# Three units of FFN2's weight sums on GpSimd in the chunk loop, and an eighth pair of strips by the seven-product scheme

## The chip, the cores and the metric

The kernel runs on one core of a Trainium2 chip. The metric is the device time of one execution in microseconds (us), as the median of several runs. TensorE (PE in the profile) multiplies, VectorE (DVE) and ScalarE (ACT) work on whole tiles, GpSimd (POOL) does a few small operations, and SyncE (SP) issues nearly all DMA transfers, in the order of its queue.

## The reference

One layer of a hybrid decoder over 1024 tokens with 1024 channels, all in float32: a SwiGLU half-step, a mixer of three parallel branches (an RWKV-7 recurrence, sliding-window attention, cross-attention into memory tokens) merged by gates, and a second SwiGLU half-step.

```python
def swiglu(u, w_in, w_out):
    gate, up = jnp.split(u @ w_in, 2, axis=-1)
    return (jax.nn.silu(gate) * up) @ w_out

f1 = swiglu(rms_norm(h, ffn1_pre_g[l]), ffn1_w_in[l], ffn1_w_out[l])
h = h + HALF_STEP * rms_norm(f1, ffn1_post_g[l])
u = rms_norm(h, mix_pre_g[l])
p_rwkv, p_swa, q_mem, gate_logits = _split(u @ w_in[l], IN_SIZES)
y_a = rwkv7_mix(p_rwkv, ...)
y_b = sliding_window_gqa_sinks(q_s, k_s, v_s, swa_sinks[l])
y_c = memory_cross_attention(q_mem.reshape(B, S, MEM_HEADS, MEM_HEAD_DIM), mem_n, mem_w_kv[l])
g_a, g_b, g_c = _split(jax.nn.sigmoid(gate_logits + gate_b[l]), (D, D, D))
merged = (g_a * (y_a @ w_branch[l, 0]) + g_b * (y_b @ w_branch[l, 1])
          + g_c * (y_c @ w_branch[l, 2]))
h = h + rms_norm(merged @ w_out[l], mix_post_g[l])
f2 = swiglu(rms_norm(h, ffn2_pre_g[l]), ffn2_w_in[l], ffn2_w_out[l])
h = h + HALF_STEP * rms_norm(f2, ffn2_post_g[l])
```

## The kernel before

**Products.** Every float32 matrix product is made of three matmuls on operands that are split in a high and a low part (`mm3`, L378 to L380): high by high, high by low, low by high. A weight tile (`w_raw`, 128x512, loaded by SP at L292) is split by a cast on ACT (`w_hi`, L301) and a subtraction on DVE (`w_lo`, L303). `plan` lists all weight operands in the order of use, and each is loaded and split some tiles ahead.

**The seven-product scheme.** A strip is 128 output columns of a projection. A plain strip takes 2 token halves x 8 blocks of 128 channels x 3 matmuls (`gate_block`, PSUM banks `pgate`). `win_pair` makes two strips at once by a Strassen-like scheme: 7 products of 4 blocks each on sums of the input (`mix_form`, products t1 to t4) and of the weights, on the banks `px`, `py` and `pz`, with `kept` copying partial sums to SBUF on ACT (`part`, L1437). `WIN_PAIRS` lists the pairs. FFN1 and FFN2 use such schemes too; for FFN2's output weights the sums of the weights are made in 11 units (q = 0 to 10) of four tiles: four loads, four DVE operations (L669 to L672), four stores to `ffn_sum_d` (`sums_beside`, on tiles named `gin`). A unit is taken up by `unit()` at the end of a gate in `filling`.

**The stages around the change.** The mixer's strips are projected, the last of them in pairs. Then comes the chunk loop of the recurrence (`rwkv_chain`, 16 chunks of 64 tokens), whose small matmuls depend on each other; gates 10 and 11 fill PE's gaps there. For each chunk SP loads `f` (640 KB) and `dinv`, POOL copies part of `f` into `gz` (L1230) and multiplies the state by the chunk's decay (`sw`, L1297), PE makes `z`, DVE copies it out of PSUM (`z`, `uv`) and makes the next state (`ts`, then `sv` at L1314 out of `ts` and `sw`). The dictionary `beside` puts further loads on SP behind the `dinv` loads of a chunk: the memory attention's `km`, `vm` and `qm`. `rwkv_finish` normalises the recurrence's output (squares `ysq` on POOL, `yrs`, `gup`). Then the memory attention runs in 8 blocks (`MemoryBlock`: scores `msc`, maxima and sums `mst` on DVE, exponentials `mp` on ACT, transposes `mptr` on PE), and the window attention; `filling` gives gates 12 to 23 and then the branch products (`pb`, weights `in_wb`) to PE wherever an attention block waits. The branch inputs are loaded as `yin` and split into `y` on ACT and DVE; the last branch's are loaded behind its window blocks.

**What sets the order.** A recording layer writes each engine's queue in one order ahead of time. `issue_after(x)` puts an instruction behind x in that order, `high_priority` ahead of others, and `keep_in_program_order` holds it to the code's. Within an engine's queue nothing overtakes.

Of the kernel before, what the change touches and what calls it, by code (L numbers as in the profile page):

```python
# [11 lines left out]
F32 = mybir.dt.float32  # L12
F32R = mybir.dt.float32r
I32 = mybir.dt.int32
ALU = mybir.AluOpType
# [3 lines left out]
P = 128  # L19
# [8 lines left out]
KP = KF // 2  # L28
OUT_FORMS = (("b11", 0), ("b21", 1), ("t2", "s2"), ("t3", "s3"), ("t4", 3), ("t1", "s1"), ("b22", "s4"))
B_FORM = {b: i for i, (b, _) in enumerate(OUT_FORMS)}  # L30
SUMS = ("s1", "s2", "s3", "s4")
# [7 lines left out]
NPAIR = 4  # L39
MAIN_PSUM = ("po", "px", "py", "pr", "pgate", "pq", "pb", "pw")  # L40
OPS = 8
KEEP = KP - OPS
RAWS = 5
SCRATCH = 1024
FORM_TILES = {"ffn1": 8, "ffn2": 12}
KH = KD // 2
# [3 lines left out]
CORNER = (4, 4)  # L50
GATES_FIRST = 10
GATES_EARLY = 12
LUMPS = (29, 52)
# [8 lines left out]
C = 64  # L62
# [170 lines left out]
class Builder:  # L233
# [430 lines left out]
    def sums_made(self, f, q, a, behind):  # L664
# [8 lines left out]
        for n, t in zip(SUMS, (a22, a11, a21, a12)):  # L673
            nc.sync.dma_start(self.sum_d[f][SUMS.index(n), q], t)

    def sums_beside(self):

        for q in range(KP):
            a = [t[:, i * TH : (i + 1) * TH].rearrange("p (k c) -> p k c", c=P) for t in (self.wide(), self.wide()) for i in (0, 1)]
            self.sums_loads("ffn2", q, a)  # L680
            yield
            self.sums_made("ffn2", q, a, self.split_last)

    def unit(self):
        if self.units:
            next(self.units, None)
# [521 lines left out]

    def rwkv_chain(self, pool, early, fetched, pk_d, inv_d, y, beside):
        nc = self.nc  # L1210
        V, S, G = nc.vector, nc.scalar, nc.gpsimd
        lo, hi = slice(0, 64), slice(64, 128)
        ROWS = (lo, hi)
# [6 lines left out]
        tile = lambda tag, shape, bufs=2: pool.tile([P] + shape, F32, tag=tag, name=tag, bufs=bufs)  # L1220
# [52 lines left out]
        n = load(0)  # L1273
# [7 lines left out]
        for c in range(NC_):  # L1281
            last = c == NC_ - 1
            nxt = None if last else load(c + 1)
            if c in beside:
                with self.tc.issue_after(self.asked.ins):
                    beside[c]()
            wc = self.wc[:, c, :].rearrange("p n -> p n ()")

            ps = self.psum("z")
            for p, q in pairs:  # L1290
                q = 1 - q
# [4 lines left out]
            for q in (0, 1):  # L1296
                G.tensor_tensor(sw[ROWS[q]], n["sv"][ROWS[q], q], wc[ROWS[q]].broadcast_to([64, NPAIR, C]), ALU.mult)  # L1297
            py = out(c - 1, before) if c else self.psum("y")
# [5 lines left out]
            if not last:  # L1304
# [3 lines left out]
                for p, q in pairs:  # L1308
                    q = 1 - q
# [179 lines left out]
    def filling(self, u, pool, gate_d, y_d):  # L1489

        for g in range(GATES_EARLY, 22):
            ps = {h: self.psum("pgate") for h in (0, 1)}
            yield from self.project_steps(self.strip("win", 24 + g), u, ps)
            self.gate_out(g, ps, pool, gate_d)
            self.unit()

# [259 lines left out]
    def mixer(self, u, cp, close_raws, att_d, gate_d, km_d, vm_d):  # L1756
# [23 lines left out]
        with tc.tile_pool(reuse_waits="tile", name="gates", bufs=2) as gp:  # L1780
# [33 lines left out]
            blocks = [MemoryBlock(self, None, b, att_d=att_d, km=km, vm=vm, ahead=ahead, y_d=y_d[2]) for b in range(nb)]  # L1814
            beside = {3: lambda: nc.sync.dma_start(km, km_d), 5: lambda: nc.sync.dma_start(vm, vm_d), 7: blocks[0].load, 8: blocks[1].load}
            with chunks, tc.tile_pool(reuse_waits="tile", name="chain", bufs=2) as pool:
                y = pool.tile([P, NPAIR, T], F32, name="y", bufs=1)
                last = self.rwkv_chain(pool, early, fetched, pk_d, inv_d, y, beside)
                with tc.issue_after(self.opened.ins):
                    for g in range(GATES_FIRST, GATES_EARLY):  # L1820
                        self.gate_block(g, u, gp, gate_d)
                self.held = []
                self.fills, self.missing = self.filling(u, gp, gate_d, y_d), 0
                self.fill(8, self.solved)
                last()
                self.rwkv_finish(pool, early, y, bonus_d, y_d[0])
            with stay, tc.tile_pool(reuse_waits="tile", name="att", bufs=1) as ap, tc.tile_pool(name="attw", bufs=2) as pool:
# [261 lines left out]
```

## Time and profile before

| | |
|---|---|
| median of 3 runs | 2253.84 us (2252.64 to 2255.07) |
| the profiled execution | 2256.49 us, its span 2254.8 us |
| mean granted TensorE clock | 0.997 |
| PE busy | 2227.1 us, 99% |
| DVE busy | 1642.5 us, 73% |
| ACT busy | 1029.6 us, 46% |
| POOL busy | 81.3 us, 4% |

The span runs from the first to the last instruction of the profiled execution. Busy times are shares of that span. In a timeline a row has the start, the length, the engine, the line and the operation with output and inputs, a count of like neighbours (x2), and in brackets the time the engine stood before it and what released it. In the list of waits stand engine and line, what was waited for, the time in us, how often, and the longest.

### The profile page before, as it was taken

The numbers are of one execution on the slowest core, as the hardware profiler recorded it, in microseconds if no ns is written. First come the engines' busy times: TensorE is split into PE (matmuls) and PEld (weight loads), VectorE is DVE, ScalarE is ACT, GpSimd is POOL, SyncE is SP. The second block draws the span as 40 slices with busy tenths as digits, with TensorE's granted clock in tenths as the row PEclk, the third lists the DMA queues.
The fourth block names the chain that finished last, engine by engine and source line by source line (L and its number), as shares of the span: only waits on it lengthen the run. The fifth ranks groups of instructions, "written<-read, shape, count | busy, mean of one in ns | idle before, by whom it ended". The sixth has DMA issues, their size and how long they took to land.

```text
span 2254.8 us, 34592 instructions
## 1 busy us (share of the span) xinstructions
PE 2227.1 (99%) x12304; PEld 1830.2 (81%) x12304; DVE 1642.5 (73%) x2761; ACT 1029.6 (46%) x1935; POOL 81.3 (4%) x154
## 2 busy tenths in 40 slices
PE   8999999999999999999999999999999999999998
PEld 6888888888887788887878887788888888888887
DVE  6988777766698887863667577684898886656576
ACT  6623333454556654444445455334663233345451
POOL 0000000000000011001330000000000000000000
PEclk9999999999999999999999999999999999999999
DMA  8565566686665456455537786654565652357663
GB/s 291 176 201 169 200 212 216 225 294 207 192 210 187 124 150 209 158 166 181 175 100 255 240 297 206 215 178 143 175 212 175 195 190 100 114 165 247 209 194 120
DMA packets 272237, 432.43 MB, mean 192 GB/s; under 512 B 50848, under 2 KB 89760, under 8 KB 271808
## 3 DMA queue, kind: packets, MB, share of 16 engines
q1 hardware_dynamic: 255968, 402.09, 55.4%
q10 hardware_dynamic: 14816, 27.07, 3.5%
q8 instruction: 97, 1.59, 0.3%
q0 software_dynamic: 1280, 1.05, 0.2%
q14 instruction: 76, 0.62, 0.1%
HBM read 292.75 MB, written 136.31 MB: 190 GB/s over the span
## 4 chain that ended last, share of the span: by engine, by line
PE 92%; DVE 4%; DMA 2%; ACT 1%; issue 1%; SPq 0%; ACTq 0%; DVEq 0%
PE px L378 9%; PE px L380 9%; PE px L379 9%; PE po L378 6%; PE po L379 6%; PE po L380 6%; PE pz L378 4%; PE pz L379 4%; PE pz L380 4%; PE pgate L378 2%; PE pgate L379 2%; PE pgate L380 2%; PE pb L378 2%; PE pb L379 2%; PE pb L380 2%; PE pr L378 2%
## 5 line engine op out<-in xcount | busy, mean ns | idle before, releaser
L301 ACT CAST w_hi<-w_raw 128x512 fp32r<-128x512 f32 x608 | 376.0, 620 | 717.6 <-PE px L379 184.7
L303 DVE TENSOR_TENSOR w_lo<-w_raw,w_hi 128x512 fp32r<-128x512 f32 x608 | 417.2, 688 | 180.0 <-ACT w_hi L301 164.3
L380 PE MATMUL po<-u,w_lo 128*128 128x512 f32 (+1 forms) x476 | 181.0, 380 | 0.0
L379 PE MATMUL po<-u,w_hi 128*128 128x512 f32 (+1 forms) x476 | 180.9, 380 | 0.0
L378 PE MATMUL po<-u,w_hi 128*128 128x512 f32 (+1 forms) x476 | 180.9, 380 | 0.0
L378 PE MATMUL px<-u,w_hi 128*128 128x512 f32 x380 | 148.0, 390 | 0.8 <-DVE km L1614 0.8
L378 PE MATMUL pz<-u,w_hi 128*128 128x512 f32 x380 | 148.1, 390 | 0.0
L380 PE MATMUL px<-u,w_lo 128*128 128x512 f32 x380 | 148.0, 389 | 0.0
L379 PE MATMUL px<-u,w_hi 128*128 128x512 f32 x380 | 147.8, 389 | 0.0
L379 PE MATMUL pz<-u,w_hi 128*128 128x512 f32 x380 | 147.8, 389 | 0.0
L380 PE MATMUL pz<-u,w_lo 128*128 128x512 f32 x380 | 147.8, 389 | 0.0
L378 PE MATMUL px<-f,w_hi 128*128 128x512 f32 x352 | 137.0, 389 | 0.0
L380 PE MATMUL px<-f,w_lo 128*128 128x512 f32 x352 | 137.0, 389 | 0.0
L379 PE MATMUL px<-f,w_hi 128*128 128x512 f32 x352 | 136.9, 389 | 0.0
L487 DVE TENSOR_TENSOR u<-hid,u 128x512 fp32r<-128x512 f32 x114 | 78.2, 690 | 50.3 <-ACT u L486 49.1
L378 PE MATMUL pgate<-u,w_hi 128*128 128x512 f32 x256 | 104.1, 407 | 0.0
L379 PEld LDWEIGHTS po<-u,w_hi 128*128 128x128 f32 x476 | 89.5, 188 | 17.1
L380 PEld LDWEIGHTS po<-u,w_lo 128*128 128x128 f32 x476 | 89.5, 188 | 17.1
L378 PEld LDWEIGHTS po<-u,w_hi 128*128 128x128 f32 x476 | 89.5, 188 | 16.8
L379 PE MATMUL pgate<-u,w_hi 128*128 128x512 f32 x256 | 102.0, 399 | 0.0
L486 ACT CAST u<-hid 128x512 fp32r<-128x512 f32 x114 | 70.5, 620 | 69.0 <-DMA hid<-form_d 60.1
L380 PE MATMUL pgate<-u,w_lo 128*128 128x512 f32 x256 | 100.5, 392 | 0.0
(454 smaller groups left out, 5184.7 us busy)
## 6 DMA issues: line engine op xcount, KB each, us to landing
w_raw<-in_ffn_in SPq DMA_DIRECT2D x224, 256.0 KB
hid<-form_d SPq DMA_DIRECT2D x154, 256.0 KB
w_raw<-in_win SPq DMA_DIRECT2D x112, 256.0 KB
form_d<-g SPq DMA_DIRECT2D x88, 256.0 KB
w_raw<-ffn_sum_d SPq DMA_DIRECT2D x88, 256.0 KB
form_d<-h SPq DMA_DIRECT2D x66, 256.0 KB
w_raw<-in_ffn_out SPq DMA_DIRECT2D x66, 256.0 KB
first_d<-first SPq DMA_DIRECT2D x48, 256.0 KB
```

The lines of the kernel that those rows point to most:

```text
L301: self.nc.scalar.copy(hi, x)
L303: self.split_last = self.nc.vector.tensor_tensor(lo, x, hi.bitcast(F32), ALU.subtract)
L378: mm(out, wh, xh, start=first, stop=False, **kw)
L379: mm(out, wh, xl, start=False, stop=False, **kw)
L380: self.last_mm = mm(out, wl, xh, start=False, stop=last, **kw)
L486: self.nc.scalar.copy(hi, x)
L487: self.nc.vector.tensor_tensor(lo, x, hi.bitcast(F32), ALU.subtract)
```

## The change

There are three parts. `GATES_FIRST` goes from 10 to 12 and `GATES_EARLY` from 12 to 14: gates 10 and 11 become an eighth pair ahead of the loop, gates 12 and 13 take their place in the loop, and `filling` starts with gate 14. Units 0 to 2 of FFN2's weight sums move into the chunk loop: their loads stand behind the `dinv` loads of chunks 1, 5 and 9, one GpSimd operation follows `sw` in each of chunks 2 to 13, and the stores come in chunks 6, 10 and 14. Units 3 to 10 stay on DVE; in `filling` they start with the end of gate 16 (before: with every gate, the first ones without effect as long as no units were set up). The loads of `km`, `vm` and `qm` move to chunks 3, 7, 11 and 12. The tiles of the finish get a pool of their own in the memory that the loop's sums have left, so its first `bo_in` loads, ahead of the loop before, come after the last stores.

```diff
@@ -40,6 +40,7 @@
 MAIN_PSUM = ("po", "px", "py", "pr", "pgate", "pq", "pb", "pw")
 OPS = 8
 KEEP = KP - OPS
+LOOP_UNITS = 3
 RAWS = 5
 SCRATCH = 1024
 FORM_TILES = {"ffn1": 8, "ffn2": 12}
@@ -48,8 +49,8 @@
 ATT_BLOCKS = (18, 19, 14, 15, 16, 17, 20, 21, 22, 23)
 GATES_PLAIN = 2
 CORNER = (4, 4)
-GATES_FIRST = 10
-GATES_EARLY = 12
+GATES_FIRST = 12
+GATES_EARLY = 14
 LUMPS = (29, 52)
 FINISH = (16, 6, 10)
 MIX_SUMS = ("t2", "t1", "t3", "t4")
@@ -673,9 +674,28 @@
         for n, t in zip(SUMS, (a22, a11, a21, a12)):
             nc.sync.dma_start(self.sum_d[f][SUMS.index(n), q], t)
 
+    def sums_in_loop(self, pool):
+
+        beside, behind = {}, {}
+        G = self.nc.gpsimd.tensor_tensor
+
+        def unit(q, c):
+            a = a11, a12, a21, a22 = [pool.tile([P, KH, P], F32, tag="ws", name="ws", bufs=8) for _ in range(4)]
+            steps = ((a22, a21, a22, ALU.add), (a21, a11, a21, ALU.subtract), (a11, a22, a11, ALU.subtract), (a12, a12, a11, ALU.subtract))
+            for n, t in enumerate(a):
+                self.nc.sync.dma_start(t, self.io["ffn2_out"][n, q])
+            for n, x in enumerate(steps):
+                behind[c + 1 + n] = lambda x=x: G(*x)
+            beside.setdefault(c + 5, []).append(lambda: [
+                self.nc.sync.dma_start(self.sum_d["ffn2"][SUMS.index(n), q], t) for n, t in zip(SUMS, (a22, a11, a21, a12))])
+
+        for q in range(LOOP_UNITS):
+            beside.setdefault(4 * q + 1, []).append(lambda q=q: unit(q, 4 * q + 1))
+        return beside, behind
+
     def sums_beside(self):
 
-        for q in range(KP):
+        for q in range(LOOP_UNITS, KP):
             a = [t[:, i * TH : (i + 1) * TH].rearrange("p (k c) -> p k c", c=P) for t in (self.wide(), self.wide()) for i in (0, 1)]
             self.sums_loads("ffn2", q, a)
             yield
@@ -1206,7 +1226,7 @@
             self.asked = S.dma_start(n["d"][q * 64 : q * 64 + 64], inv_d[c, :, q].rearrange("p s t -> s p t"))
         return n
 
-    def rwkv_chain(self, pool, early, fetched, pk_d, inv_d, y, beside):
+    def rwkv_chain(self, pool, early, fetched, pk_d, inv_d, y, beside, behind):
         nc = self.nc
         V, S, G = nc.vector, nc.scalar, nc.gpsimd
         lo, hi = slice(0, 64), slice(64, 128)
@@ -1281,9 +1301,9 @@
         for c in range(NC_):
             last = c == NC_ - 1
             nxt = None if last else load(c + 1)
-            if c in beside:
-                with self.tc.issue_after(self.asked.ins):
-                    beside[c]()
+            with self.tc.issue_after(self.asked.ins):
+                for f in beside.get(c, ()):
+                    f()
             wc = self.wc[:, c, :].rearrange("p n -> p n ()")
 
             ps = self.psum("z")
@@ -1294,7 +1314,10 @@
             V.tensor_copy(z, v3(ps))
             sw = tile("sw", [NPAIR, C])
             for q in (0, 1):
-                G.tensor_tensor(sw[ROWS[q]], n["sv"][ROWS[q], q], wc[ROWS[q]].broadcast_to([64, NPAIR, C]), ALU.mult)
+                scaled = G.tensor_tensor(sw[ROWS[q]], n["sv"][ROWS[q], q], wc[ROWS[q]].broadcast_to([64, NPAIR, C]), ALU.mult)
+            if c in behind:
+                with self.tc.issue_after(scaled.ins):
+                    behind[c]()
             py = out(c - 1, before) if c else self.psum("y")
 
             for p, q in pairs:
@@ -1492,7 +1515,8 @@
             ps = {h: self.psum("pgate") for h in (0, 1)}
             yield from self.project_steps(self.strip("win", 24 + g), u, ps)
             self.gate_out(g, ps, pool, gate_d)
-            self.unit()
+            if g >= GATES_EARLY + 2:
+                self.unit()
 
         yin = lambda: self.yin.tile([P, TH], F32, tag="yin", name="yin", bufs=4)
         load = lambda i: self.load_y(y_d[i], (self.u_tile, self.u_tile), yin)
@@ -1812,10 +1836,13 @@
             vm = ahead.tile([P, 2, 512], F32, name="vm_in")
             nb = T // P
             blocks = [MemoryBlock(self, None, b, att_d=att_d, km=km, vm=vm, ahead=ahead, y_d=y_d[2]) for b in range(nb)]
-            beside = {3: lambda: nc.sync.dma_start(km, km_d), 5: lambda: nc.sync.dma_start(vm, vm_d), 7: blocks[0].load, 8: blocks[1].load}
             with chunks, tc.tile_pool(reuse_waits="tile", name="chain", bufs=2) as pool:
                 y = pool.tile([P, NPAIR, T], F32, name="y", bufs=1)
-                last = self.rwkv_chain(pool, early, fetched, pk_d, inv_d, y, beside)
+                with tc.tile_pool(reuse_waits="tile", name="loop_sums", bufs=8) as loop_pool:
+                    beside, behind = self.sums_in_loop(loop_pool)
+                    for c, f in ((3, lambda: nc.sync.dma_start(km, km_d)), (7, lambda: nc.sync.dma_start(vm, vm_d)), (11, blocks[0].load), (12, blocks[1].load)):
+                        beside.setdefault(c, []).append(f)
+                    last = self.rwkv_chain(pool, early, fetched, pk_d, inv_d, y, beside, behind)
                 with tc.issue_after(self.opened.ins):
                     for g in range(GATES_FIRST, GATES_EARLY):
                         self.gate_block(g, u, gp, gate_d)
@@ -1823,7 +1850,8 @@
                 self.fills, self.missing = self.filling(u, gp, gate_d, y_d), 0
                 self.fill(8, self.solved)
                 last()
-                self.rwkv_finish(pool, early, y, bonus_d, y_d[0])
+                with tc.tile_pool(reuse_waits="tile", name="finish", bufs=3) as finish_pool:
+                    self.rwkv_finish(finish_pool, early, y, bonus_d, y_d[0])
             with stay, tc.tile_pool(reuse_waits="tile", name="att", bufs=1) as ap, tc.tile_pool(name="attw", bufs=2) as pool:
                 cos = ap.tile([P, T], F32, name="cos")
                 sin = ap.tile([P, T], F32, name="sin")
```

**PE, the last pairs ahead of the chunk loop.** The last number of a name is its buffer: `px_9877` is a PSUM bank, `mix_form_8271` the last block of t2, `mix_form_8281` the first of t3. Before, in the last pair:

```order
4417 L378 MATMUL px_9877<-mix_form_8271,w_hi_9668 128x512
4418 L379 MATMUL px_9877<-mix_form_8272,w_hi_9668 128x512
4419 L380 MATMUL px_9877<-mix_form_8271,w_lo_9670 128x512
4420 L378 MATMUL px_9877<-mix_form_8281,w_hi_9770 128x512
4421 L379 MATMUL px_9877<-mix_form_8282,w_hi_9770 128x512
```

Now, in the last pair but one:

```order
4420 L381 MATMUL px_9863<-mix_form_8271,w_lo_9670 128x512
4421 L380 MATMUL px_10022<-u_5953,w_hi_9876 128x512
4422 L381 MATMUL px_10022<-u_5952,w_lo_9878 128x512
4423 L379 MATMUL px_10022<-u_5958,w_hi_9876 128x512
4424 L380 MATMUL px_10022<-u_5959,w_hi_9876 128x512
4425 L381 MATMUL px_10022<-u_5958,w_lo_9878 128x512
4426 L379 MATMUL px_9863<-mix_form_8281,w_hi_9770 128x512
```

Five matmuls of the next pair have come between t2 and t3, which write the same bank; in the last pair 11 of t1 stand there.

**POOL, the start of the chunk loop.** The rows are `gz` copies, `sw` multiplies and the new weight sums `ws`. Before, then now:

```order
35 L1297 TENSOR_TENSOR sw<-sv,wc 64x256 x4
36 L1230 COPY gz<-f 64x4x64 x2
37 L1297 TENSOR_TENSOR sw<-sv,wc 64x256 x2
38 L1230 COPY gz<-f 64x4x64 x2
39 L1297 TENSOR_TENSOR sw<-sv,wc 64x256 x2
```

```order
35 L1317 TENSOR_TENSOR sw<-sv,wc 64x256 x4
36 L1250 COPY gz<-f 64x4x64 x2
37 L1317 TENSOR_TENSOR sw<-sv,wc 64x256 x2
38 L688 TENSOR_TENSOR ws<-ws 128x512
39 L1250 COPY gz<-f 64x4x64 x2
40 L1317 TENSOR_TENSOR sw<-sv,wc 64x256 x2
41 L688 TENSOR_TENSOR ws<-ws 128x512
42 L1250 COPY gz<-f 64x4x64 x2
```

One `ws` has come in behind each chunk's `sw` and ahead of the next chunk's `gz` copies, twelve in all.

**DVE, block 6 of the memory attention.** `gin` are weight sums, `mst` the maxima of the block's scores. Before, then now:

```order
1344 L303 TENSOR_TENSOR w_lo<-w_raw,w_hi 128x512
1345 L669 TENSOR_TENSOR gin<-gin 128x512
1346 L203 TENSOR_REDUCE mst<-msc 128x2 x2
1347 L670 TENSOR_TENSOR gin<-gin 128x512
1348 L205 TENSOR_SCALAR mst<-mst 128x4
```

```order
1353 L304 TENSOR_TENSOR w_lo<-w_raw,w_hi 128x512
1354 L670 TENSOR_TENSOR gin<-gin 128x512
1355 L671 TENSOR_TENSOR gin<-gin 128x512
1356 L204 TENSOR_REDUCE mst<-msc 128x2
1357 L672 TENSOR_TENSOR gin<-gin 128x512
1358 L204 TENSOR_REDUCE mst<-msc 128x2
1359 L673 TENSOR_TENSOR gin<-gin 128x512
1360 L206 TENSOR_SCALAR mst<-mst 128x4
```

The unit at this place is q = 4 before and q = 6 now; its four sums now all stand ahead of the `mst` operation that the exponentials wait for, where it was two.

## The prediction

> **What bounds the kernel now.** I read the page first: the share of each engine, then the chain that ended last.
>
> ```profile
> span 2254.8 us, 34592 instructions
> PE 2227.1 (99%) x12304; PEld 1830.2 (81%) x12304; DVE 1642.5 (73%) x2761; ACT 1029.6 (46%) x1935; POOL 81.3 (4%) x154
> PE 92%; DVE 4%; DMA 2%; ACT 1%; issue 1%; SPq 0%; ACTq 0%; DVEq 0%
> ```
>
> TensorE (PE) is busy for 99% of the span and carries 92% of the chain. So a matmul that disappears shortens the span by one matmul, work on another engine counts only where PE stands for it, and GpSimd (POOL) at 4% has room. Next, the waits of PE, longest first, to see how much standing time there is to win at all:
>
> ```profile
> PE pq L1527 <- DMA mkv<-in_mkv_k: 6.5, 1, 6.5
> PE mptr L105 <- ACT mp L208: 3.1, 1, 3.1
> ...
> PE px L378 <- ACT part L1437: 1.0, 1, 1.0
> ```
>
> The first is the kernel's start, which this change leaves alone. The second lies in the memory attention, the third in the last pair of strips; both places are touched.
>
> **Term 1, the eighth pair.** As the seven-product scheme, two strips take 7 products x 4 blocks x 3 matmuls = 84 of 128x512; as two plain gates they took 2 strips x 2 halves x 8 blocks x 3 = 96. Twelve matmuls go. What one costs is read from PE's timeline in the last pair, not from the 0.39 us of an instruction, since neighbours overlap:
>
> ```profile
> 1043.62 0.39 PE L379 MATMUL py<-u,w_hi 128*128 128x512 f32 x1
> ...
> 1049.29 0.39 PE L380 MATMUL px<-mix_form,w_lo 128*128 128x512 f32 x1
> 1050.64 0.50 PE L378 MATMUL px<-mix_form,w_hi 128*128 128x512 f32 x1 [0.97 <-ACT part L1437]
> ```
>
> There are 25 steps from the first row to the second: (1049.29 - 1043.62) / 25 = 0.227 us. Term 1 is -12 x 0.227 = **-2.7 us**.
>
> **Term 2, the stall at the last pair.** The third row above starts 1.35 us after its neighbour. Before, product t3 followed product t2 on the same PSUM bank px at once, and t3 had to wait until ACT had copied px away:
>
> ```profile
> 1049.49 0.62 ACT L301 CAST w_hi<-w_raw 128x512 fp32r<-128x512 f32 x1 [2.10 <-PE px L379]
> 1050.01 0.58 ACT L1437 COPY part<-px 128x512 f32<-128x512 f32 x1
> ```
>
> With one more pair the order changes: between t2 and t3 stand 5 matmuls in the last pair but one and 11 in the last (the order shows it). Five matmuls give 5 x 0.227 = 1.13 us, and the stall to be covered is 1.35 - 0.23 = 1.12 us; eleven give 2.5 us. I take **-1.1 us**, with 0 as the other end if the copy slips behind one more cast of 0.62 us.
>
> The pair also brings three more weight tiles to split, each with such a cast on ACT and a subtraction on DVE, by the page's group:
>
> ```profile
> L303 DVE TENSOR_TENSOR w_lo<-w_raw,w_hi 128x512 fp32r<-128x512 f32 x608 | 417.2, 688 | 180.0 <-ACT w_hi L301 164.3
> ```
>
> Four weight sums of that DVE size come in the FFN1 stage, and copies of partial sums on ACT. DVE's 73% and ACT's 46% leave room for them, **0 us**; without that cover they would cost 3 x (0.62 + 0.69) + 4 x 0.69 = 6.7 us. The loop gets as many gates as filler as before, gates 12 and 13 for 10 and 11.
>
> **Term 3, the loop with sums on GpSimd.** Twelve tensor operations of 128x512 are put on POOL, one per chunk in chunks 2 to 13, behind the `sw` multiply and ahead of the `gz` copies. A chunk's timeline before, POOL, then DVE, then PE:
>
> ```profile
> 1080.92 2.06 POOL L1297 TENSOR_TENSOR sw<-sv,wc 64x256 f32<-64x256 f32 x2 [3.92 <-DVE sv L1314]
> 1083.04 0.83 POOL L1230 COPY gz<-f 64x256 f32<-64x256 f32 x2
> 1087.52 1.53 POOL L1297 TENSOR_TENSOR sw<-sv,wc 64x256 f32<-64x256 f32 x2 [3.64 <-DVE sv L1314]
> ```
>
> ```profile
> 1081.82 0.69 DVE L303 TENSOR_TENSOR w_lo<-w_raw,w_hi 128x512 fp32r<-128x512 f32 x1
> 1082.42 0.42 DVE L1294 COPY z<-z 128x256 f32<-128x256 f32 x1
> 1083.80 0.86 DVE L1303 COPY uv<-z 64x256 f32<-64x256 f32 x2 [0.96 <-PE z L1219]
> 1087.03 0.86 DVE L1314 TENSOR_TENSOR sv<-ts,sw 64x256 f32<-64x256 f32 x2
> ```
>
> ```profile
> 1088.12 0.69 PE L1219 MATMUL z<-sv,gz 128*64 128x64 f32 x16
> ```
>
> A chunk lasts 1087.52 - 1080.92 = 6.6 us, and POOL idles 3.6 to 3.9 us of it. The nearest POOL operation of this shape, `ysq` in the finish, took 1.49 us. `sw` would end at about 1083, the sum at 1084.5, the `gz` copies at 1085.3; `gz` is first used at 1088.12, so 2.8 us are left, and the next `sw` at 1087.52 finds POOL free. DVE next: where POOL and DVE both work on tiles in SBUF, they hold each other up, as the finish shows:
>
> ```profile
> 1181.74 1.49 POOL L1336 TENSOR_TENSOR ysq<-y 128x512 f32<-128x512 f32 x1 [3.41 <-DVE ysq_lo L1338]
> ```
>
> ```profile
> 1180.98 0.68 DVE L1338 TENSOR_TENSOR ysq_lo<-ysq,ysq_hi 128x512 fp32r<-128x512 f32 x1
> ...
> 1182.24 1.53 DVE L1338 TENSOR_TENSOR ysq_lo<-ysq,ysq_hi 128x512 fp32r<-128x512 f32 x1
> ```
>
> The same operation took 0.68 us alone and 1.53 beside it: 0.85 us per meeting. In the stretch that the sum takes, 1083 to 1084.5, DVE has only `z` and `uv`, which read PSUM, and now and then a `w_lo`, which is made well ahead of its use. So I take **0 us**; the lower end is 0, since the loop holds no PE stall to win, and the upper is a meeting on the path in every chunk, 12 x 0.85 = +10.2 us. I choose 0 since `sv`, the two-tile DVE operation on the path, starts 2.5 us after the sum's end.
>
> The Trainium skill, page "SBUF — State Buffer", section "🔬 SBUF: two separate sides", has a rule for this: DVE with two SBUF inputs and a GpSimd operation that reads SBUF compete for one pair of ports, and whoever comes second waits for the other's whole instruction. The two finish rows agree (1.53 for 0.68 us); a DVE copy out of PSUM has no two SBUF inputs, so by the rule too term 3 would be 0.
>
> The loads and stores of the three units, 12 + 12 of 256 KB on SP, each go behind the `dinv` load of a chunk:
>
> ```profile
> 1060.00:1160.00 100.00, 99.42 (x1821) 83.21 (x1818) 62.72 (x157) 42.12 (x102) 34.09 (x58) 1.00 0.51 156
> ```
>
> ```profile
> 1083.37 0.76 SPq L1204 DMA_DIRECT2D f<-pk_d  x1
> 1084.23 1.24 SPq L1206 DMA_DIRECT2D dinv<-inv_d  x2
> ...
> 1089.96 0.33 SPq L1204 DMA_DIRECT2D f<-pk_d  x1
> ```
>
> SP is free from 1085.5 to 1089.96; four issues at the 0.62 us of a `dinv` end by 1088.0, so the next `f` isn't issued later. On the DMA engines the loop moves 156 GB/s at a share of 0.51, so they could do about 306 GB/s; a chunk with an extra 4 x 262 KB carries 156 x 6.6 + 1049 = 2079 KB, 6.8 us at that rate, 0.2 us more than a chunk lasts. `f` is issued 6.2 us ahead of its first reader (the `gz` copies a chunk later, 1083.04 + 6.6), and may come 0.2 us later, so I put 0 here. Without that cover, six chunks would lose 0.2 us each, 1.2 us. The units start from data loaded a chunk and more earlier (loads behind chunk 1, 5, 9, first step behind the `sw` of the next), so POOL shouldn't stand for them.
>
> **Term 4, the attention.** Twelve `gin` sums leave DVE, and 24 transfers leave this stretch. Only where PE waited for DVE does it pay: the 3.1 us wait of `mptr`. DVE's and SP's timelines show its root:
>
> ```profile
> 1257.20 0.17 DVE L205 TENSOR_SCALAR mst<-mst 128x4 f32<-128x4 f32 x1
> 1261.22 0.69 DVE L669 TENSOR_TENSOR gin<-gin 128x512 f32<-128x512 f32 x1 [3.85 <-DMA gin<-in_ffn_out]
> ...
> 1274.15 0.69 DVE L669 TENSOR_TENSOR gin<-gin 128x512 f32<-128x512 f32 x1 [7.39 <-DMA gin<-in_ffn_out]
> 1274.76 1.28 DVE L203 TENSOR_REDUCE mst<-msc 128x2 f32<-128x512 f32 x2
> ...
> 1276.56 0.16 DVE L205 TENSOR_SCALAR mst<-mst 128x4 f32<-128x4 f32 x1
> ```
>
> ```profile
> 1261.94 4.59 SPq L674 DMA_DIRECT2D ffn_sum_d<-gin  x4
> 1266.58 0.42 SPq L655 DMA_DIRECT2D gin<-in_ffn_out  x1
> ...
> 1267.67 1.12 SPq L655 DMA_DIRECT2D gin<-in_ffn_out  x2
> ```
>
> ```profile
> 1274.24 0.60 PE L105 MATMUL mptr<-ident,mp 128*128 128x128 f32 x4
> 1277.91 0.66 PE L105 MATMUL mptr<-ident,mp 128*128 128x128 f32 x4 [3.07 <-ACT mp L208]
> ```
>
> A weight sum stands in DVE's queue ahead of the softmax maximum of block 6, its `gin` loads were issued at 1266.58 to 1268.8, behind stores that could go only when the sums that began at 1261.22 were done, and DVE stood 7.39 us; exponentials and transposes came after. In the new order that unit is still there (unit 6 instead of 4), with two sums, not one, ahead of the first reduction and four ahead of the `mst` that ACT waits for: from the load's landing to `mst` 2.4 us before (1274.15 to 1276.56), about 3.7 us now (four sums of 0.69 and 1.28 us of reductions, less overlap). Against this, the unit before it has its first reduction ahead of its first sum, and its loads no longer stand behind other transfers: they should land about 3 us sooner, by the 3.85 us wait at 1261.22, and all that follows with them. I take the middle of -3.1 and +1, rounded to the side of the shorter queue: **-1.2 us**.
>
> **Term 5, the last branch.** The attention has two gates fewer to fill its gaps (14 to 21 instead of 12 to 21) and takes branch matmuls in their place: 66 of them (15 us) are left between the last window product and the last branch instead of 165 (37.5 us). The loads of the last branch's input then come behind the weight tile of operand 26, not 21, on SP.
>
> ```profile
> 1433.58 6.41 SPq L1708 DMA_DIRECT2D yin<-y_d  x4
> ```
>
> ```profile
> 1446.50 0.69 DVE L487 TENSOR_TENSOR y<-yin,y 128x512 fp32r<-128x512 f32 x1
> ```
>
> ```profile
> 1476.01 0.39 PE L378 MATMUL pb<-y,w_hi 128*128 128x512 f32 x1
> ```
>
> Before, first issue to last split took 1447.2 - 1433.6 = 13.6 us and ended 29 us ahead of need. Five weight tiles of 24 matmuls are 5 x 24 x 0.227 = 27 us, which takes nearly all of it: some 2 us remain. **0 us**, upper end +3 if the loads take the 4 to 5 us longer that a busy queue has cost elsewhere (3.85 above).
>
> **Sum.** -2.7 - 1.1 + 0 - 1.2 + 0 = -5.0 us. The profiled execution took 2256.49 us, 2.65 above the median 2253.84, with 1.7 us outside its span; so its span would be 2249.8, its time 2251.5, and the median 2248.8, say **2249.0 us**. Runs of this kernel differ by less than 0.2% (4.5 us), which I take as the limit of "no change": faster means below 2249.3.
>
> **Rivals.** (a) The `gin` wait stays or moves to the next block: for it speaks that the new order puts more sums ahead of `mst`, against it the shorter queue; -2.7 - 1.1 + 0 to +1 = 2250 to 2251. (b) The last branch starves: for it the 2 us left of 29; -5 + 1 to +3 = 2250 to 2252. (c) The change is slower: each sum on POOL pushes `sv` or `ts` of its chunk, by a `w_lo` that it blocks and that then pushes DVE's chain; at 0.85 us in each of twelve chunks, -5 + 10.2 = +5.2, 2259. It outweighs the gain from 0.42 us a chunk on (12 x 0.42 = 5.0) and is measurably slower from 0.8. For it speaks that DVE's `sv` ends close to PE's need (`sv` 1087.03 to 1087.9, PE at 1088.12); against it, that a `w_lo` ran beside `sw` at 1081.82 in 0.69 us while it was `sw` that took 2.06 for 1.53, and the 6.6 us stayed. (d) The saved matmuls don't come off the span, since the added pair waits for its weight sums or its forms: no net change, 2254; against it, PE ran through the seven pairs with the one stall shown.
>
> By the rule of the Trainium skill named above, (c) needs a two-input DVE operation in each sum's 1.5 us; only the trace after can show one.
>
> **Chances.** The sum as forecast or a little better 0.45; (a) 0.20; (b) 0.10; (c) 0.17, of which a half at less than its full price; (d) 0.08. The forecast's case holds 2245.5 (all of the 3.1 us and small stalls of the finish gone) to 2250. Faster 0.45 (some of the first case ends within 0.2%, and some of (a) below it, which cancels), same 0.39 with (a), (b), (d) and a little of (c), slower 0.16. The range reaches from 2245.0 to 2257.5, in the middle of (c).
>
> **What would show it.** Right: PE with 84 more `px`, `py`, `pz` matmuls and 96 fewer `pgate`; no wait `px <- ACT part` near 1.0; chunks still 6.6 us apart with `ws` of 1.0 to 1.5 us on POOL; `mptr <- ACT mp` below 2 us; `pb` without a wait for `y`. Wrong: chunks of 7 us or more, a PE wait for `sv`, `gz` or `f` in the loop, a long DVE wait for `gin` with PE behind it, or a `pb` wait for the last branch's split.

## Result and the profile after

| | before | after |
|---|---|---|
| median, runs of the first comparison | 2254.96 us (9 runs, 2252.1 to 2258.87) | 2249.47 us (9 runs, 2247.14 to 2250.59) |
| ratio to before, 95% interval | | 0.9978 (0.9969 to 0.9986), some -5.0 us |
| second comparison (after_2) | 2254.07 us (20 runs) | 2248.37 us (7 runs), ratio 0.9971 (0.996 to 0.9982) |
| profiled execution, span | 2254.8 us | 2247.8 us |

The change is faster by 5.0 us in the first comparison (interval -7.0 to -3.2) and by 6.5 us in the second (-9.0 to -4.1); 2249.0 was forecast. The prediction called faster what lies more than 4.5 us below before. Both gains do, but both intervals reach above that line, and the nine runs of before spread over 6.8 us, more than the 4.5 taken for it. From the page of the changed kernel, and from the list of PE's waits (columns: what was waited for, us in total, times, longest):

```profile
span 2247.8 us, 34587 instructions
PE 2224.2 (99%) x12292; PEld 1828.0 (81%) x12292; DVE 1641.3 (73%) x2759; ACT 1032.2 (46%) x1941; POOL 97.0 (4%) x166
```

```profile
PE pq L1551 <- DMA mkv<-in_mkv_k: 6.6, 1, 6.6
PE ss L1014 <- DVE n_lo L488: 1.8, 1, 1.8
PE ps_rs L474 <- ACT sq_hi L468: 1.3, 3, 0.6
```

Twelve matmuls are gone (12304 to 12292), and POOL has twelve instructions and 15.7 us more. The two waits that stood in the attention (`mptr`, 3.1 us) and in the last pair (`px`, 1.0 us) are in the list no more.

The last pair on PE, in the timeline after (the matmuls' line numbers are one higher than before):

```profile
1067.72 0.39 PE L381 MATMUL px<-mix_form,w_lo 128*128 128x512 f32 x1
1067.94 0.39 PE L380 MATMUL pz<-mix_form,w_hi 128*128 128x512 f32 x1
...
1070.44 0.39 PE L379 MATMUL px<-mix_form,w_hi 128*128 128x512 f32 x1
```

t2 ends with the first row, eleven matmuls of t1 follow on `pz`, and t3 starts on `px` at 1070.44: 12 steps in 2.72 us, 0.227 us each, no wait. A chunk of the loop, POOL and then DVE:

```profile
1100.57 2.05 POOL L1317 TENSOR_TENSOR sw<-sv,wc 64x256 f32<-64x256 f32 x2 [2.92 <-DVE sv L1337]
1102.70 1.27 POOL L688 TENSOR_TENSOR ws<-ws 128x512 f32<-128x512 f32 x1
1103.91 0.84 POOL L1250 COPY gz<-f 64x256 f32<-64x256 f32 x2
1107.15 1.53 POOL L1317 TENSOR_TENSOR sw<-sv,wc 64x256 f32<-64x256 f32 x2 [2.39 <-DVE sv L1337]
```

```profile
1101.46 0.69 DVE L304 TENSOR_TENSOR w_lo<-w_raw,w_hi 128x512 fp32r<-128x512 f32 x1
...
1103.43 0.86 DVE L1326 COPY uv<-z 64x256 f32<-64x256 f32 x2 [0.95 <-PE z L1239]
```

The sum `ws` fits into POOL's idle time, which is now 2.4 to 2.9 us a chunk, and the chunk lasts 1107.15 - 1100.57 = 6.58 us. `uv` keeps its 0.86 us beside `ws`. Where this `w_lo` meets `sw`, it is `sw` that grows to 2.05 us, as before. In one chunk of the twelve it is the other way round: a `w_lo` at 1127.96 took 1.00 us behind `sw`, the `ws` behind it 1.60 us, and the chunk was 6.58 us long all the same.

The last branch (SP, then DVE's first and last split of its first half, then PE's first matmul on it):

```profile
1452.25 1.84 SPq L1732 DMA_DIRECT2D yin<-y_d  x4
```

```profile
1458.49 0.69 DVE L488 TENSOR_TENSOR y<-yin,y 128x512 fp32r<-128x512 f32 x1 [0.30 <-ACT y L487]
...
1462.10 0.68 DVE L488 TENSOR_TENSOR y<-yin,y 128x512 fp32r<-128x512 f32 x1
```

```profile
1468.86 0.39 PE L379 MATMUL pb<-y,w_hi 128*128 128x512 f32 x1
```

From first issue to last split it is 10.5 us, and 6 us are left.

### The profile page after: what moved, and what is told of

The parts are those of the page before. It is cut to its first block, busy times and chain, and to the rows that moved or that the text cites. A ratio compares the mean times of both kernels' runs of the same rounds, so it can differ in the third digit from the quotient of the medians.

```text
span 2247.8 us, 34587 instructions
## 1 busy us (share of the span) xinstructions
PE 2224.2 (99%) x12292; PEld 1828.0 (81%) x12292; DVE 1641.3 (73%) x2759; ACT 1032.2 (46%) x1941; POOL 97.0 (4%) x166
## 4 chain that ended last, share of the span: by engine, by line
PE 93%; DVE 4%; DMA 1%; ACT 1%; issue 1%; SPq 0%; DVEq 0%; ACTq 0%
PE px L379 9%; PE px L381 9%; PE px L380 9%; PE po L379 6%; PE po L380 6%; PE po L381 6%; PE pz L379 4%; PE pz L381 4%; PE pz L380 4%; PE pgate L379 2%; PE pgate L380 2%; PE pgate L381 2%; PE pb L379 2%; PE pb L381 2%; PE pb L380 2%; PE pr L379 2%
## 5 line engine op out<-in xcount | busy, mean ns | idle before, releaser
L379 PE MATMUL pgate<-u,w_hi 128*128 128x512 f32 x224 | 90.5, 404 | 0.0
L380 PE MATMUL pgate<-u,w_hi 128*128 128x512 f32 x224 | 88.9, 397 | 0.0
L379 PE MATMUL pr<-u,w_hi 128*128 128x512 f32 x224 | 87.6, 392 | 0.0
```

The lines of the kernel that those rows point to most:

```text
L379: mm(out, wh, xh, start=first, stop=False, **kw)
L380: mm(out, wh, xl, start=False, stop=False, **kw)
```

## Experiments

Times are ratios to the kernel before, run on the same chip, with 95% intervals; 0.001 is 2.25 us.

**One part at a time.** `pair_alone` has the eighth pair without the loop's sums, `sums_alone` the reverse. Both keep the moved loads of `km`, `vm` and `qm` and the finish's own pool, which were not tried alone.

```diff
# pair_alone, against the changed kernel
-LOOP_UNITS = 3
+LOOP_UNITS = 0
-            if g >= GATES_EARLY + 2:
-                self.unit()
+            self.unit()
# sums_alone, against the changed kernel
-GATES_FIRST = 12
-GATES_EARLY = 14
+GATES_FIRST = 10
+GATES_EARLY = 12
-            if g >= GATES_EARLY + 2:
+            if g >= 16:
```

> The eighth pair without the loop's sums: all 11 units of FFN2's weight sums are again made by VectorE in the attention, in the order that the eight gates left as filler allow. Theory (the terms add up): -2.7 us for the twelve matmuls and -1.1 us for the wait of px, both seen before the loop, and none of the 3.1 us wait of mptr is sure to go, since in this order three sums in a row stand ahead of a maximum in one block: 2250 to 2252 us where before has 2254 to 2255, with a wait mptr <- ACT mp of 0 to 4 us. Rival (the gain comes from the sums on GpSimd, the pair is eaten up by its weight sums and copies): within 1 us of before, with a new wait of px or pz ahead of the loop.

> The three units on GpSimd in the loop, without the eighth pair: gates 10 and 11 fill the loop as before. Theory: the wait of px (1.0 us) stays, the twelve matmuls stay, the loop's chunks stay at 6.58 to 6.60 us, and the wait of mptr (3.1 us) goes because no weight sum with late loads stands ahead of block 6's maxima: -3.1 us, 2251 to 2252 where before has 2254 to 2255. Rival 1 (the sums on GpSimd cost something in the loop that the pair hid): chunks longer than 6.65 us. Rival 2 (the mptr wait went by the pair's new order): mptr still waits 2 to 4 us, and the time is that of before.

Measured: `pair_alone` 0.9992 (0.9983 to 1.0), -1.8 us, median 2253.54, above the 2250 to 2252 that were expected; `sums_alone` 0.9989 (0.998 to 0.9998), -2.5 us, median 2251.89 as expected. From the waits of PE, `pair_alone` first:

```profile
PE mptr L106 <- ACT mp L209: 3.4, 2, 2.9
PE ss L1014 <- DVE n_lo L488: 1.4, 1, 1.4
...
PE pv L103 <- DVE sc L137: 0.6, 1, 0.6
```

```profile
PE ps_rs L453 <- DVE rs_lasty L451: 1.2, 1, 1.2
PE px L379 <- ACT part L1460: 1.0, 1, 1.0
```

The two gains add up to -4.3 us, inside the first interval of the whole (-7.0 to -3.2), so the times don't show whether the parts need each other; the traces say more. With all eleven units still in the attention and two gates fewer to cover them, `pair_alone` has lost the `px` wait and got a wait of `mptr` in another block, so in its trace most of the 3.8 us is given back there. DVE didn't stand in that block; it had the window attention's sine tables and weight sums to do, and ACT stood 1.80 us for `mst`, then loaded a table (1.28 us) ahead of the exponentials. `sums_alone` keeps the `px` wait and has no `mptr` wait. DVE's waits for `gin` loads go with the sums: 11.5 us in before, 12.2 in `pair_alone`, 2.4 in the changed kernel, none in `sums_alone`. Rivals 1 and 2 of the second expectation fall (no longer chunks, no `mptr` wait). The first expectation's rival is right on the time, since the medians differ by only 0.7 us, and wrong on the place: nothing new waits ahead of the loop.

**The wait of px alone.** `apart` is the kernel before with the last pair's products held to the code's order:

```diff
-            self.win_pair(len(WIN_PAIRS) - 1, fs, out, att_d, gate_d)
+            self.win_pair(len(WIN_PAIRS) - 1, fs, out, att_d, gate_d, lambda: self.last_mm)
```

> The kernel before, with one thing changed: in the last pair the products are held to the code's order, so that the 12 matmuls of t1 (bank pz) stand between t2 and t3 (bank px). Theory (the 1.0 us wait of px is a reuse of one bank without work between): the row px <- ACT part goes, the step of 1.35 us there becomes 0.23, all else as before: -1.1 us, which the times alone can't show (0.05%). Rival (the copy on ACT is late for other reasons): the wait stays near 1 us somewhere in the last pair. The run is also a second look at the attention of before: if the wait of mptr (3.1 us) belongs to the kernel and not to one execution, it is again between 2.5 and 4 us.

Measured: 0.9991 (0.9982 to 0.9999), -2.0 us, which the times can't tell from the 1.1 expected. In the trace the `px` row is gone, and `mptr` waited 1.5 us, not 3.1:

```profile
PE pq L1527 <- DMA mkv<-in_mkv_k: 6.4, 1, 6.4
PE mptr L105 <- ACT mp L208: 1.5, 1, 1.5
```

So the `px` wait is the bank's reuse, and work between removes it. The `mptr` wait isn't a fixed number, which the next pair of runs was for.

**The same two kernels again.** `before_2` and `after_2` are unchanged copies.

> The kernel before, unchanged, profiled again, to see how far its longest wait in the attention is the same in every execution. Theory (it hangs on when the gin loads land): mptr <- ACT mp between 1 and 4 us, px <- ACT part again 1.0 us. Rival (it is fixed by the order): 3.1 us within 0.2.

> The changed kernel, unchanged, profiled again and timed on this chip: no wait of mptr above 1 us, no px <- ACT part, time 2247 to 2251 us, 4 to 7 us below before.

Measured: `before_2` took 2251.95 us, with `px` at 1.0 us again and no wait of `mptr` at this place, where 1 to 4 us were expected; `after_2` as expected (table above). In three executions of this attention the wait was 3.1, 1.5 and 0 us. It goes with the time that DVE stood for the first `gin` of unit 4: 7.39 us in before (the prediction's row), then in `apart` and in `before_2`:

```profile
1272.86 0.69 DVE L669 TENSOR_TENSOR gin<-gin 128x512 f32<-128x512 f32 x1 [5.82 <-DMA gin<-in_ffn_out]
```

```profile
1271.61 0.69 DVE L669 TENSOR_TENSOR gin<-gin 128x512 f32<-128x512 f32 x1 [4.25 <-DMA gin<-in_ffn_out]
```

Where DVE stood 1.57 us less, PE waited 1.58 us less (3.07 to 1.49), and another 1.57 us less took the rest. The price shows in PE's own rows: from the start of `mpv` to that of the next `msc` PE took 10.28 us in before (1272.46 to 1282.74), 7.14 in `apart` (1272.74 to 1279.88) and 5.56 in `before_2` (1273.06 to 1278.62). So the wait of 1.5 us cost 1.6, and that of 3.1 us cost 4.7; the difference is the clock (last section). What releases the wait shows in ACT's timeline of the first trace of before:

```profile
1276.84 0.47 ACT L208 ACTIVATE mp<-msc,mst 128x256 f32<-128x256 f32 x1 [10.21 <-DVE mst L205]
1277.21 0.19 ACT L208 ACTIVATION_READ_ACCUMULATOR mp<-msc,mst 128x1 f32 x1
1277.30 0.47 ACT L208 ACTIVATE mp<-msc,mst 128x256 f32<-128x256 f32 x1
1277.66 0.20 ACT L208 ACTIVATION_READ_ACCUMULATOR mp<-msc,mst 128x1 f32 x1
```

`mptr` went on at 1277.91, right after the fourth of these rows: they empty the first `msc` bank, which holds two heads. The transposes at that time belong to the block before, and what they wait for is a bank: the scores, transposes and values of the attention share four (`psum`, tag "bg"). When the `gin` loads land early enough, the maxima come in time and nothing is seen. The changed kernel at these places:

```profile
1278.33 0.69 DVE L670 TENSOR_TENSOR gin<-gin 128x512 f32<-128x512 f32 x1 [2.36 <-DMA gin<-in_ffn_out]
1278.94 0.68 DVE L204 TENSOR_REDUCE mst<-msc 128x2 f32<-128x512 f32 x1
...
1286.51 0.69 DVE L670 TENSOR_TENSOR gin<-gin 128x512 f32<-128x512 f32 x1
```

DVE stood 2.36 us for unit 5, and not at all for unit 6, where before it had stood 3.85 and 7.39 us for the units at these places.

**How much GpSimd can take.** Two or three more operations of the same size follow each sum, into a tile that nobody reads; in `on_dve` the twelve sums go to DVE.

```diff
# pool_x3 (range(2)) and pool_x4 (range(3))
+        dump = pool.tile([P, KH, P], F32, tag="dump", name="dump", bufs=1)
-                behind[c + 1 + n] = lambda x=x: G(*x)
+                behind[c + 1 + n] = lambda x=x: [G(*x)] + [G(dump, x[1], x[2], x[3]) for _ in range(2)]
# on_dve
-        G = self.nc.gpsimd.tensor_tensor
+        G = self.nc.vector.tensor_tensor
```

> The changed kernel with each of GpSimd's twelve sums followed by two more operations of the same size into a tile that nobody reads: GpSimd's chunk is then 1.53 + 3 x 1.27 + 0.84 = 6.2 us of 6.58. Theory (GpSimd's queue has room until its own work fills the chunk, and sums and VectorE's operations on the path do not meet): chunks of 6.58 us, the time of the changed kernel within 1 us. Rival (each meeting with a VectorE operation of two SBUF inputs costs 0.85 us): the sums now reach to the sv of the next chunk, so 12 x 0.85 = 10 us, chunks of 7.4 us, 2259 us.

> As with three operations per chunk, now three extra ones after each sum: GpSimd's chunk is 1.53 + 4 x 1.27 + 0.84 = 7.4 us or, with lengthened operations, up to 7.8, which is more than the 6.58 us of a chunk. Theory (GpSimd's queue is what bounds its use): the twelve chunks last 7.4 to 7.8 us, the loop grows by 10 to 15 us, about 2260 to 2264 us. Rival (something else, such as the meetings with VectorE, sets the limit): chunks well above 7.8 us, or below 7.2.

> The changed kernel with the twelve sums of the loop on VectorE instead of GpSimd, at the places that the order gives them: most stand between gz and z or between z and uv, which PE waits for. Theory (VectorE is on the loop's path, GpSimd isn't): each sum of 0.69 us that stands ahead of z or uv lengthens its chunk by 0.4 to 0.6 us, 12 of them by 4 to 7 us: 2253 to 2257 us. Rival (VectorE idles 37% of the loop and takes them in): 2249 to 2250 us, chunks of 6.58 us.

Measured: `pool_x3` 0.9979 (0.997 to 0.9989), as the change itself; `pool_x4` 1.0039 (1.0024 to 1.0053), +8.8 us, median 2262.91 of three runs, as expected; `on_dve` 0.9988 (0.9979 to 0.9997), -2.7 us, median 2251.68, below the 2253 to 2257 that were expected. A chunk of `pool_x3` and one of `pool_x4` on POOL:

```profile
1101.67 1.27 POOL L690 TENSOR_TENSOR ws<-ws 128x512 f32<-128x512 f32 x1
1103.01 2.63 POOL L690 TENSOR_TENSOR dump<-ws 128x512 f32<-128x512 f32 x2
1105.58 0.93 POOL L1252 COPY gz<-f 64x256 f32<-64x256 f32 x2
1106.59 1.36 POOL L1319 TENSOR_TENSOR sw<-sv,wc 64x256 f32<-64x256 f32 x2
1108.03 1.26 POOL L690 TENSOR_TENSOR ws<-ws 128x512 f32<-128x512 f32 x1
```

```profile
1124.71 1.29 POOL L1319 TENSOR_TENSOR sw<-sv,wc 64x256 f32<-64x256 f32 x2
...
1132.46 1.75 POOL L1319 TENSOR_TENSOR sw<-sv,wc 64x256 f32<-64x256 f32 x2
```

And the waits of PE in `pool_x4` and in `on_dve`:

```profile
PE z L1241 <- POOL gz L1252: 11.2, 10, 1.4
```

```profile
PE z L1239 <- DVE sv L1337: 2.8, 3, 1.2
```

With three operations POOL is all but full: in the chunk shown it has no gap and a chunk (`ws` to `ws`, 1108.03 - 1101.67) lasts 6.4 us; others last up to 7.2, and in eight of the twelve POOL stands 0.36 us for `sv`. With four, eight of eleven chunks last 7.75 us (1132.46 - 1124.71) and the rest up to 8.4, and PE waits for `gz` in ten of them: POOL's queue is the bound, for the most part by its own work. The meetings count for little beside it: with three operations POOL still works when DVE makes `sv`, and that pair of operations grew from 0.86 to 0.99 and 1.10 us in these chunks, not by 0.85. In all the loop of `pool_x3` was some 1.6 us longer, so its chunks were not 6.58 us but 6.7, which its times can't tell. In `on_dve` PE waits 2.8 us for `sv`: three chunks lengthened (7.4 to 7.9 us), in the first of which two sums in a row stood ahead of `ts` and `sv` and waited 0.82 us for their loads, and the other sums fitted DVE's idle time. Its median lies 2.2 us above the change, with intervals that overlap, so by the times alone GpSimd isn't shown to be better than DVE here; the size lies between theory and rival.

**A ninth pair.** `ninth` also makes gates 12 and 13 a pair; `ninth_a` gives each attention block less filler besides.

```diff
# ninth, against the changed kernel
-GATES_FIRST = 12
-GATES_EARLY = 14
+GATES_FIRST = 14
+GATES_EARLY = 16
-            if g >= GATES_EARLY + 2:
-                self.unit()
+            self.unit()
# ninth_a: that, and
-LUMPS = (29, 52)
+LUMPS = (26, 46)
```

> The changed kernel with a ninth pair (gates 12 and 13) and gates 14 and 15 in the loop, gates 16 to 23 left as filler. Twelve more matmuls go: -2.7 us. But the attention now uses up every other branch matmul, none is left between the last window product and the last branch. Theory (term 5's slack of some 6 us in the changed kernel's trace is used up): in the changed kernel the last branch's first input was split 5.0 to 8.7 us after the last window product, so PE now waits 4 to 9 us there: +1 to +6 us net, 2251 to 2255. Rival (the loads come earlier by themselves): a wait below 2 us, 2247 to 2248 us.

> The ninth pair, and fewer filler matmuls for each attention block (LUMPS 26 and 46 instead of 29 and 52), so that 36 matmuls (8.2 us) are left between the last window product and the last branch. Theory: the wait of the last branch is 0 to 1 us, the twelve matmuls pay -2.7 us, and the shorter fill costs nothing as long as each block's softmax is done in time: 2246 to 2247.5 us, the fastest so far. Rival (the attention's blocks need the fill they had): waits of ptr, mptr, pv or mpv for ACT or DVE, some tenths of a us to 2 us in several blocks, 2249 us or more.

Measured: `ninth` 1.0047 (1.0034 to 1.006), +10.6 us, median 2264.49, far above the 2251 to 2255 that were expected; `ninth_a` 1.0005 (0.9995 to 1.0014), median 2254.69. Both are slower than the change. From PE's waits, then SP and PE in `ninth`:

```profile
PE pb L379 <- ACT y L487: 5.9, 2, 4.1
PE pb L379 <- DVE u L1766: 4.3, 5, 1.9
PE mptr L106 <- ACT mp L209: 2.8, 2, 1.6
```

```profile
1475.20 0.33 SPq L293 DMA_DIRECT2D w_raw<-in_wb  x1
1475.62 1.80 SPq L1731 DMA_DIRECT2D yin<-y_d  x4
```

```profile
1475.12 0.65 PE L103 MATMUL pv<-pt,vd 128*64 128x256 f32 x4
1479.86 0.49 PE L379 MATMUL pb<-y,w_hi 128*128 128x512 f32 x1 [4.08 <-ACT y L487]
...
1483.19 0.79 PE L379 MATMUL pb<-y,w_hi 128*128 128x512 f32 x1 [1.80 <-ACT y L487]
```

Behind the last weight tile in SP's queue, the loads go out only when the window attention is over. That is rival (b) of the prediction, one pair further on, and it gives the first of the three rows. The expectation had this wait and not the others: branch products brought forward waited for DVE, which itself stood 3.7 us for gate loads (`gin<-gate_d`), and DVE's waits for the sums' loads are back at 20.7 us. `ninth_a` has no wait at the last branch, but its attention now waits 2.1 us at a `pv`, with four weight sums, the first of which stood 2.88 us for its load, ahead of the softmax in DVE's queue; the time is that of before. Its expectation of 2246 to 2247.5 us was wrong. So with the sums where they are, eight pairs are the most of the settings tried; others of `LUMPS`, or more units in the loop, were not tried.

**A wait put in.** Operations on DVE delay a block's maxima in the changed kernel:

```diff
+        if self.b == 5:
+            dump = self.pool.tile([P, 512], F32, tag="dump", name="dump", bufs=1)
+            V.memset(dump, 0.0)
+            V.tensor_scalar(dump[:, 0:4], st[:, 0], 0.0, None, ALU.mult)
+            for _ in range(3):      # wait7: range(7)
+                V.tensor_tensor(dump, dump, dump, ALU.add)
+            V.tensor_tensor(st[:, 0], st[:, 0], dump[:, 0:4], ALU.add)
```

> The changed kernel with a wait put into it: in memory block 5 three VectorE operations of 128x512 (0.69 us each, on a tile of zeros, added to the maxima as 0) stand between the maxima and the exponentials, some 2.5 us in all. PE then waits 1 to 2.5 us at mptr, depending on the block's slack. Theory (a short stand of PE costs its length, a long one also lowers the granted clock: 0.64 over 4 us after 3.1 us in the trace of before, 1.00 after 1.5 us in the run with t1 between): below 2 us no lower clock, the stretch from the first msc to the last mptr grows by the wait alone. Rival (a wait costs its length, whatever it is): the same here, so this run is the base for the longer one.

> The same with seven operations, some 5 us in all: PE waits 3.5 to 5 us at mptr of block 5. Theory (clock): the granted clock behind the wait falls to 0.6 to 0.7 for some 4 us, and the stretch from the first msc to the last mptr grows by the wait and 2 us more. Rival (length alone; what before lost besides was DMA or VectorE work): the stretch grows by the wait within 0.3 us, clock at 1.00.

Measured: `wait3` 0.9988 (0.9979 to 0.9998), `mptr` waited 1.3 us, with the clock at 1.00 (last section); `wait7` 0.998 (0.9969 to 0.999), no wait, where 3.5 to 5 us were expected. The trace of `wait3` is of its fastest run (2249.84); its median of 2252.0 lies 3.6 us above `after_2`, more than the wait in the trace, and why the others lost more isn't shown. In `wait7` the transposes got the bank that `yo` had emptied:

```profile
1281.75 0.66 PE L106 MATMUL mptr<-ident,mp 128*128 128x128 f32 x4 [0.28 <-ACT yo L1731]
```

So the longer delay (seven operations, 5.0 us) cost PE no wait, since the exponentials weren't in the way. This failed as a test of long waits, and shows again that the wait is one for a bank.

## Why the prediction was right

- **Term 1, -2.7 us: held.** 84 matmuls for 96, in the same step of 0.227 us.
- **Term 2, -1.1 us: held.** The wait was 1.0 us in the three traces that kept the pair's old order (before, `before_2`, `sums_alone`) and absent where t1 stands between.
- **Term 3, 0 us: held**, with chunks of 6.58 us and `ws` of 1.27 us, not the 1.49 of `ysq`. The DMA engines carried it:

```profile
1080.00:1180.00 100.00, 99.48 (x1818) 83.21 (x1814) 63.19 (x158) 42.30 (x102) 48.94 (x71) 1.00 0.69 218
```

  Their share rose from 0.51 to 0.69, and no wait for `f` came. Rival (c) doesn't hold: neither the sums nor three times as many operations held up DVE by 0.85 us a chunk. Nor does rival (d), since the pair brought no new wait ahead of the loop. On the Trainium skill's rule (page "SBUF — State Buffer", section "🔬 SBUF: two separate sides"): `uv`, which reads PSUM, kept its 0.86 us beside `ws`, as by the rule; that `sw` went from 1.53 to 2.05 us at a `w_lo` fits the rule with POOL as the one that waits: the second of its two operations started at 1101.49, just behind the `w_lo` at 1101.46. At 1127.96 the `w_lo` started second, behind a `sw` of 1127.81, and it was the `w_lo` that grew.
- **Term 4, -1.2 us: the place and the cause were right, the size was partly luck.** The wait was taken as a property of the order, 3.1 us in every execution, that would move by some part. It differs from execution to execution (3.1, 1.5, 0 us), and where it is long it costs more than its length (last section): 4.7, 1.6 and 0 us in the three traces, 2.1 as their mean, and all of it is gone in both traces of the changed kernel. Moving the sums alone, which removes this wait, gave -2.5 us (-4.5 to -0.5). The forecast of -1.2 lies in that interval too, but it was reached as the middle of -3.1 and +1, and the clock was not in it. The sums ahead of `mst` did no harm, for the loads came earlier, as argued: the changed kernel's DVE stood 2.36 us at the unit before and not at this one.
- **Term 5, 0 us: held**, with 6 us left instead of 2, since the loads took 10.5 us and not 13.6. `ninth` shows what lies behind the slack.
- **Sum.** -2.7 - 1.1 - 2.5 = -6.3 us, with terms 3 and 5 at 0: within both measured intervals (-7.0 to -3.2, and -9.0 to -4.1), and so is the forecast of -5.0. The times can't tell the two apart, and that 2249.0 came within half a us of the first median is partly luck. The two profiled spans can be added up: 2.7 + 1.1 + 4.7 = 8.5 us, less 1.5 that the changed kernel's execution lost in its first 35 us, ahead of all that was changed (the four `ps_rs` matmuls on `rsy` start at 33.44 before and at 34.97 now), is 7.0, the difference of the spans.

## What to carry to other kernels

Work that fills another engine's waits is a stock: the eighth pair took two gates out of the attention and came to 1.8 us alone, and to 2.5 or 4.0 us beside the sums' move (the intervals overlap); with the ninth the attention and the last branch waited. Give an idle engine what fits its idle time in one period of the loop, count its queue from end to end, and expect little cost until it is full (here 1.6 us over twelve chunks at 6.4 of 6.6 us, some 13 us beyond). A wait that hangs on when a transfer lands should be read in several traces before it is put into a sum.

## What the runs showed of the hardware

A stand of PE can halve the clock behind it. In these traces the granted clock is either 1.00 or 0.50, and apart from the kernel's start and end a stretch at 0.50 lasts 3.41 us, or twice that in `ninth`. The changes in one run lie whole multiples of 3.413 us apart (in `ninth_a` 783.43 and 1377.35, 174 of them), as if on a grid. A window laid across a change shows a mixture, so the windows here follow the grid (PE busy, PEld, DVE, ACT, POOL, then the granted clock, DMA share and GB/s). Before, around the wait of 3.1 us:

```profile
1275.69:1279.10 3.41, 1.19 (x8) 1.06 (x8) 2.66 (x7) 2.27 (x9) 0.00 (x0) 1.00 0.47 179
1279.10:1282.51 3.41, 3.41 (x10) 2.63 (x9) 3.38 (x8) 1.64 (x4) 0.00 (x0) 0.50 0.61 201
1282.51:1285.93 3.42, 3.42 (x17) 2.92 (x16) 1.58 (x4) 0.25 (x1) 0.00 (x0) 1.00 0.96 286
```

And two waits of 1.8 us at `ss`, ahead of the loop, in `ninth_a` and in the changed kernel:

```profile
780.02:783.43 3.41, 1.57 (x7) 1.17 (x7) 3.34 (x5) 2.45 (x4) 2.24 (x5) 1.00 0.75 211
783.43:786.85 3.42, 3.42 (x10) 2.65 (x9) 3.41 (x5) 0.00 (x0) 0.02 (x1) 0.50 0.44 116
```

```profile
780.31:783.72 3.41, 1.60 (x8) 1.30 (x8) 3.41 (x5) 2.30 (x4) 2.26 (x5) 1.00 0.80 220
783.72:787.13 3.41, 3.41 (x17) 2.83 (x16) 3.40 (x5) 0.00 (x0) 0.00 (x0) 1.00 0.41 107
```

What one such stretch costs can be estimated as 3.41 x 0.5 = 1.7 us, and `before_2` against before bears it out (4.7 us for a wait of 3.1). How long PE stood inside one stretch of the grid (in runs without a drop counted back from the change at the end), and the clock in the next:

| run, wait | PE stood, us of 3.41 | clock next |
|---|---|---|
| `ninth`, 4.1 us, its second stretch | 2.39 | 0.50 |
| `pair_alone`, 2.9 us | 2.31 | 0.50 |
| before, 3.1 us | 2.22 | 0.50 |
| `ninth_a`, 2.1 us | 2.08 | 0.50 |
| `ninth`, 4.1 us, its first stretch | 1.92 | 1.00 |
| `ninth_a`, 1.8 us at `ss` | 1.84 | 0.50 |
| after, 1.8 us at `ss` | 1.81 | 1.00 |
| `ninth_a`, 1.95 us at a `po` | 1.79 | 1.00 |
| `ninth`, 1.9 us at a `pb` | 1.75 | 1.00 |
| `apart`, 1.5 us | 1.49 | 1.00 |
| `wait3`, 1.3 us | 1.30 | 1.00 |

So the length of the wait alone doesn't decide: 1.95 us left the clock at 1.00 and 1.84 didn't. How much of it falls into one stretch sorts them better: above 2 us the clock always fell, below 1.8 us never, and between them (1.81, 1.84, 1.92) it went either way, so this isn't all of it. The start of the kernel and its end, where the clock is at 0.50 for the last 6 to 10 us of every run (from 2237.80 in the changed kernel), are not in the table. The Trainium skill, page "TensorE: Matmul & The Clock Gate", section "🎯 Why this matters for your kernels", advises against PE-idle gaps of more than about 3 us between bursts of matmuls; the runs agree there (three waits of 2.9 us and more in the attention and the last branch, three drops), and show drops behind two shorter waits, of 1.8 and 2.1 us. A wait of that length put in by an experiment is still missing, since the one of `wait7` didn't come about.
